# A list scheduler's rule for the port that VectorE and GpSimd share, and a new recorded order of the attention's blocks

## The chip, the core and the metric

One core of a Trainium2 chip runs one launch of the program. The metric is the device time of that launch in microseconds. Engines are named as in the profile: PE is TensorE's matmul, PEld its weight load, DVE is VectorE, ACT is ScalarE, POOL is GpSimd, SP is SyncE, which issues most of the DMAs.

## What is computed

The reference is one inference step of a two-layer decoder trunk with model width 1024, on 512 prompt positions and 8 sequences of 8 sample positions, all in float32. Cut to what matters:

```python
for l in range(DEPTH):                                   # 2 layers
    sh1, sc1, g1, sh2, sc2, g2 = ada_mod(c, ada_w[l], ada_b[l], 6)
    h = modulate(rms_norm(x, norm_g[l, 0]), sh1, sc1)
    if l < N_A_LAYERS:
        out, nbuf, h_last = recurrent_block(h, ...)      # conv, gates, linear recurrence
    else:
        q = apply_partial_rope((h @ attn_w_q[j]).reshape(B, T, N_HEADS, HEAD_DIM), pos)
        out = sliding_sink_attention(q, k_all, v_all, attn_sinks[j], p0) @ attn_w_o[j]
    x = x + g1[:, None, :] * out
    h = modulate(rms_norm(x, norm_g[l, 1]), sh2, sc2)
    x = x + g2[:, None, :] * swiglu(h, ffn_w_in[l], ffn_w_out[l])
    if l == N_A_LAYERS - 1:
        kv = (modulate(rms_norm(x, kv_norm_g), kv_shift, kv_scale) @ w_kv)   # keys, values
y = rms_norm(x, final_g)
```

## The kernel before

**Tiling.** The stream x is kept transposed in SBUF in two halves, A (h = 0) and B (h = 1); each half has 256 prompt columns and 32 sample columns, 288 in all, in 8 chunks of 128 rows. Float32 accuracy is made from three products in float32r: a value is split into hi (a rounding cast on ACT) and lo (value minus hi, a subtraction on DVE, now and then on POOL). So every weight block of 128 columns is loaded into a `raw` tile, cast by ACT into a `wh` tile and subtracted by DVE into another (`convert`, `operand`); a product of 8 row blocks is 24 matmuls of 128x288. Four `raw` tiles and ten `wh` tiles exist.

**Stages.** Recurrent block of layer 0 (about 30 to 250 us of the span), feed-forward of layer 0 (to about 640), shared keys and values (to about 690), attention with the q projection and the beginning of the output projection (about 690 to 820), rest of the output projection (to about 870), feed-forward of layer 1 and final norm (to the end). Beside these, matmuls for the conditioning vectors run in groups of 16 (tile `ada`) until about 608 us. Each feed-forward takes its first three column blocks plainly; the other 19 are done in pairs of halves with seven products where a plain product needs eight (`ffn` from line 1177, with `steps` at 1219 and `seven` at 1289). For these, POOL computes sums of weight quarters in place in `raw`: in one step S1 needs one sum, S2 two and S4 one (`operand`, which then casts on ACT and subtracts on DVE). With 19 steps in two layers these are 152 sums of 128x512 on POOL. S4 also has one product of 128x288 on POOL.

**Order of the work.** Nothing is issued while the program text runs. Each operation is recorded (`Engine.record`, lines 388 to 447; all instructions therefore stand at line 447 in the profile) with its engine, an estimated cost in ns, its operands and a `port` class. `Recorder.schedule` (from line 213) then simulates the five engines once and writes out one fixed order for each engine, which the chip follows: an engine's instructions run in that order, and each waits for its operands by semaphores. In each round the simulation takes, for every engine, the available operation with the smallest `s + 0.75 * prio`, where `s` is its simulated earliest start and `prio` its place in the recorded order, looking at up to 24 operations; of the engines' picks the one that starts first is placed. Tiles from rings (`raw`, `wh`, `sl`, `ta`, `tb`, `td`, the PSUM banks `mm` and `ada`) are given out in the same pass.

**The port.** Line 404 marks an operation that, in the model, uses a port which DVE and GpSimd share: a POOL operation that reads a wide SBUF operand, and a DVE operation that reads no PSUM and has two wide SBUF inputs or is a `tensor_scalar`. Class 1 is the usual case; class 2 (line 405) is a POOL operation of at most 40 elements. `port` holds the simulated end of the last class 1 operation (line 333). A class 1 operation on DVE may start 130 ns before that end; one on POOL starts 20 ns after it (line 302), whichever engine held the port before. So when both engines have a class 1 operation waiting behind a DVE operation, DVE's next one starts first in the simulation, and POOL's is put off again until DVE has nothing for the port.

**The attention.** `ATT` (line 53) is a list of blocks which the attention stage records one after another: `q0A` is q projection unit 0 of half A (24 matmuls and the rotary step; unit weights are converted at first use and released when both halves are done), `a0A` one chunk of two heads (4 or 8 score matmuls, masks with maximum on DVE, exponentials on ACT, a normalisation on ACT, DVE and POOL; its second part, transposes, the product with the values and a split, is put off by `flush(1)` until the next `a` or `s` block), `s0A` one sample sequence (`attn_sample`, with two DMAs for its cached keys and values), `fA` the end of a half's attention (`attn_fin`: flush, `k_out` with its small output DMAs, and the split of the sample columns that every output projection unit of that half reads), `o0A` unit 0 of the output projection. After the list come the other output units.

Of the kernel before, what the change touches and what calls it, by code (L numbers as in the profile page):

```python
# [49 lines left out]
WIN = 600  # L50

RNN = "x0 x1 x2 g0 g1 x3 y0 y1 x4 g2 g3 x5 y2 x6 y3 g4 g5 x7 y4 y5 g6 g7 y7 y6"
ATT = ("q0A q2A a0A q1A q0B a2A a1A q1B q3A a0B q2B a1B q4A a3A a4A q3B a2B q5A q4B a3B q6A a5A q5B q7A a6A a4B s0A "
       "q6B a5B s1A s2A s3A q7B a7A s0B a6B fA s2B a7B s1B o0A s3B o1A fB o2A")
LOOK = {"PE": 24, "DVE": 24, "ACT": 24, "POOL": 24, "SP": 24}
NRAW = 4
NSL, NTA, NTB, NTD = 37, 7, 8, 4
# [71 lines left out]
class Recorder:  # L129
# [83 lines left out]
    def schedule(self):  # L213
        import bisect

        last = {}
        for op in self.ops:
            for n in op.tiles:
                if n in self.kind_of:
                    last[n] = last.get(n, 0) + 1  # L220
            op.npred = len(op.preds)
            op.ready = 0.0
            for q in op.preds:
                q.succ.append(op)
        rel_at = {n: 0.0 for n in last}
        engs = ("PE", "DVE", "ACT", "POOL", "SP")
        avail = {e: [] for e in engs}
        free = {e: 0.0 for e in engs}
        slots = {k: [0.0] * c for k, (c, _) in self.kinds.items()}
        nxt = {k: 0 for k in self.kinds}  # L230
        got = set()
        cold = 0.0


        port, mode = 0.0, 0
        pos = {n: j for k in self.order for j, n in enumerate(self.order[k])}
        used = {n for n in last}
        table = [next(j for j, (n, _) in enumerate(TABLES) if n == "silu")]
        dma_free = [0.0]
        out = []  # L240

        def push(op):
            bisect.insort(avail[op.eng], (op.prio, op.i, op))

        for op in self.ops:
            if op.npred == 0:
                push(op)

        def alloc_time(op, now):
            t = 0.0  # L250
            need = {}
            for n in op.allocs:
                if n in got:
                    continue
                k = self.kind_of[n]
                sl = slots[k]
                i = need.get(k, 0)
                need[k] = i + 1
                o = self.order[k]
                while nxt[k] < len(o) and (o[nxt[k]] in got or o[nxt[k]] not in used):  # L260
                    nxt[k] += 1

                j, at = nxt[k], i
                while at and j + 1 < len(o):
                    j += 1
                    at -= o[j] not in got and o[j] in used
                m = i + (o[j] != n) * self.kinds[k][1]
                if len(sl) <= m:
                    return None
                t = max(t, sorted(sl)[m])  # L270
            return t

        n_left = len(self.ops)
        sp = deque(o.i for o in self.ops if o.eng == "SP")
        rest = deque(sorted(self.ops, key=lambda o: o.prio))
        done = set()
        while n_left:
            best = None
            while sp and sp[0] in done:
                sp.popleft()  # L280
            sp_next = sp[0] if sp else 0
            while rest[0].i in done:
                rest.popleft()
            limit = rest[0].prio + WIN
            for e in engs:
                f = free[e]
                pick = None
                seen = 0
                for pr, i, op in avail[e]:
                    if e == "SP" and i > sp_next + SPW:  # L290
                        break
                    if pr > limit:
                        break
                    at = alloc_time(op, f) if op.allocs else 0.0
                    if at is None:
                        seen += 1
                        if seen > LOOK[e]:
                            break
                        continue
                    s = max(f, op.ready, at)  # L300
                    if op.port == 1:
                        s = max(s, port - 130 if e == "DVE" else port + 20)
                    if e == "PE" and op.mode != mode:
                        s = max(s, f + 100)
                    sw = e == "ACT" and op.func and op.func not in FREE_FUNCS and (table[0] is None or op.func not in TABLES[table[0]][1])
                    if sw:
                        s = max(s, f + 1283)
                    key = (s + (SWW if sw else 0) + BETA * pr, pr)
                    if pick is None or key < pick[0]:
                        pick = (key, s, op, sw)  # L310
                    seen += 1
                    if seen > LOOK[e]:
                        break
                if pick and (best is None or pick[1] < best[1]):
                    best = pick
            if best is None:
                raise RuntimeError("no instruction can go: " + str({e: [(o.i, o.allocs) for _, _, o in avail[e][:3]] for e in engs}) + str({k: len(v) for k, v in slots.items()}))
            _, s, op, sw = best
            e = op.eng
            avail[e].remove((op.prio, op.i, op))  # L320
            if sw:
                table[0] = next(j for j, (_, fs) in enumerate(TABLES) if op.func in fs)
            for n in op.allocs:
                if n in got:
                    continue
                k = self.kind_of[n]
                c = [u for u in slots[k] if u <= s] or slots[k]
                slots[k].remove(max(c) if c is not slots[k] else min(c))
                got.add(n)
            op.start = s  # L330
            cost = op.cost
            if op.port == 1:
                port = s + cost
            elif op.port == 2 and s + 60 < port:
                cost += port - s
            if e == "PE":
                mode = op.mode
            if e == "PE":
                if s - free[e] > 3400:
                    cold = s + 3400  # L340
                if s < cold:
                    cost *= 2
            if op.lat:

                free[e] = s + op.cost
                b = max(s + op.cost + 650, dma_free[0])
                dma_free[0] = b + op.lat
                op.end = b + op.lat + 1700
            else:
                op.end = free[e] = s + cost  # L350
            for n in op.tiles:
                if n in last:
                    last[n] -= 1
                    rel_at[n] = max(rel_at[n], op.end)
                    if last[n] == 0:
                        slots[self.kind_of[n]].append(rel_at[n] + (260 if self.kind_of[n] in ("mm", "ada") or e == "PE" else 150))
            for q in op.succ:
                q.npred -= 1
                q.ready = max(q.ready, op.end + DELAY[op.eng][q.eng])
                if q.npred == 0:  # L360
                    push(q)
            out.append(op)
            done.add(op.i)
            n_left -= 1
        out.sort(key=lambda o: (o.start, o.i))
        return out
# [107 lines left out]
def trunk_kernel(ctx, tc, a):  # L474
# [1292 lines left out]
    each = []  # L1767
    for w in ATT.split():
        h, n = "AB".index(w[-1]), int(w[1:-1] or 0)
# [227 lines left out]
```

## Time and profile before

| what | before |
|---|---|
| median of 3 runs | 1275.53 us (1274.91 to 1280.13) |
| the profiled execution's own time | 1275.33 us |
| its span, first to last instruction | 1273.5 us |
| granted TensorE clock, mean | 0.993 |
| PE busy | 1246.1 us (98%) |
| PEld busy | 1172.8 us (92%) |
| DVE busy | 905.7 us (71%) |
| ACT busy | 659.4 us (52%) |
| POOL busy | 488.2 us (38%) |

All engines run at once, so the shares don't add up to one. An operation that waits for the port shows in the profile as a longer operation, not as idle time before it; an operation that waits for a semaphore shows as idle time with the engine and tile that released it.

### The profile page before, as it was taken

How to read it: one execution, taken by the hardware profiler on the slowest of the kernel's cores; microseconds unless marked ns; L12 is line 12 of the kernel's file. 1: busy time of each engine (PE TensorE's matmuls, PEld its weight loads, DVE VectorE, ACT ScalarE, POOL GpSimd, SP SyncE). 2: the span in 40 equal slices, each digit the busy share in tenths (PEclk: the TensorE clock that was granted, in tenths of full speed). 3: DMA queues.
4: the chain of work that ended last, by engine and by line, in shares of the span. 5: the costliest groups of instructions: out<-in, count | busy, mean ns of one | idle time of the engine just before them, and what ended most of it. 6: DMA issues, size and time to landing. Idle time of an engine off the chain costs nothing.

```text
span 1273.5 us, 25461 instructions
## 1 busy us (share of the span) xinstructions
PE 1246.1 (98%) x9568; PEld 1172.8 (92%) x9568; DVE 905.7 (71%) x2156; ACT 659.4 (52%) x1469; POOL 488.2 (38%) x709
## 2 busy tenths in 40 slices
PE   7999999999999999999999999999999999999997
PEld 5798899899998998999999997999999999999997
DVE  6988885775584686467578878558857758757856
ACT  4788873762352354145357768538424425524522
POOL 3476640131551552345024436110435345335511
PEclk8999999999999999999999999999999999999999
DMA  9956554416646556444432321322333323323232
GB/s 306 315 174 199 182 166 149 157 52 211 187 141 178 180 160 199 155 150 136 125 83 56 69 76 38 111 84 96 90 94 83 100 84 96 96 78 97 71 96 75
DMA packets 223981, 165.40 MB, mean 130 GB/s; under 512 B 23757, under 2 KB 209065, under 8 KB 223826
## 3 DMA queue, kind: packets, MB, share of 16 engines
q1 hardware_dynamic: 223410, 163.45, 42.5%
q8 instruction: 75, 1.23, 0.4%
q14 instruction: 48, 0.39, 0.1%
q0 software_dynamic: 448, 0.32, 0.1%
HBM read 160.85 MB, written 4.87 MB: 130 GB/s over the span
## 4 chain that ended last, share of the span: by engine, by line
PE 73%; DVE 13%; ACT 6%; POOL 4%; issue 2%; DMA 1%; SPq 0%; ACTq 0%; POOLq 0%; DVEq 0%
PE mm L447 69%; PE ada L447 4%; DVE wh L447 4%; DVE sl L447 4%; POOL raw L447 3%; ACT wh L447 2%; DVE ta L447 1%; DMA reg<-in_x_prompt_dram 1%; DVE td L447 1%; ACT tb L447 1%; ACT h L447 1%; ACT sl L447 1%; ACT ta L447 1%; DVE tb L447 1%; DVE h L447 1%
## 5 line engine op out<-in xcount | busy, mean ns | idle before, releaser
L447 PE MATMUL mm<-h,wh 128*128 128x288 f32 x4128 | 596.8, 299 | 3.5 <-ACT h L447 2.1
L447 PEld LDWEIGHTS mm<-h,wh 128*128 128x128 f32 x4128 | 562.4, 189 | 21.7 <-issue 9.9
L447 PE MATMUL mm<-sl,wh 128*128 128x288 f32 x3218 | 462.4, 296 | 0.8 <-ACT ta L447 0.8
L447 PEld LDWEIGHTS mm<-sl,wh 128*128 128x128 f32 x3218 | 436.9, 188 | 9.4 <-issue 5.9
L447 ACT CAST wh<-raw 128x512 fp32r<-128x512 f32 (+3 forms) x388 | 266.4, 710 | 292.4 <-PE mm L447 208.4
L447 DVE TENSOR_TENSOR wh<-raw,wh 128x512 fp32r<-128x512 f32 (+3 forms) x388 | 344.9, 913 | 60.1 <-ACT wh L447 54.0
L447 POOL TENSOR_TENSOR raw<-raw 128x512 f32<-128x512 f32 x76 | 109.8, 1445 | 183.9 <-DVE wh L447 154.1
L447 POOL TENSOR_TENSOR x<-x,ta 128x32 f32<-128x32 f32 x152 | 58.7, 386 | 306.8 <-DVE ta L447 306.7
L447 DVE SCALAR_TENSOR_TENSOR x<-mm,mods,x 128x256 f32<-128x256 f32 x160 | 77.3, 483 | 133.2 <-PE mm L447 132.1
L447 POOL TENSOR_TENSOR raw<-raw,raw 128x512 f32<-128x512 f32 x76 | 111.8, 1471 | 3.7
L447 PE MATMUL mm<-tb,wh 128*128 128x288 f32 (+1 forms) x488 | 89.7, 299 | 4.5 <-POOL sl L447 1.6
L447 PEld LDWEIGHTS mm<-tb,wh 128*128 128x128 f32 x488 | 72.3, 188 | 9.4 <-DVE td L447 5.4
L447 POOL TENSOR_TENSOR td<-td,td 128x288 f32<-128x288 f32 x38 | 32.0, 843 | 111.9 <-ACT td L447 106.5
L447 ACT ACTIVATE ta<-x 128x288 f32<-128x288 f32 x56 | 24.3, 443 | 67.2 <-POOL x L447 62.1
L447 PE MATMUL mm<-ta,wh 128*128 128x288 f32 (+1 forms) x254 | 55.9, 298 | 0.0
L447 DVE TENSOR_TENSOR td<-mm,td 128x288 f32<-128x288 f32 x76 | 33.2, 452 | 27.9 <-PE mm L447 27.9
L447 PE MATMUL ada<-reg,cz 128*32 128x512 f32 (+1 forms) x448 | 49.5, 553 | 0.0
L447 DVE TENSOR_TENSOR sl<-ta,sl 128x288 fp32r<-128x288 f32 x54 | 44.9, 834 | 1.7 <-ACT sl L447 1.5
L447 ACT COPY td<-mm 128x256 f32<-128x256 f32 (+1 forms) x102 | 34.2, 353 | 20.4 <-PE mm L447 18.4
L447 DVE TENSOR_TENSOR sl<-td,sl 128x288 fp32r<-128x288 f32 x50 | 38.2, 764 | 8.1 <-ACT sl L447 8.1
L447 ACT ACTIVATE ta<-mm 128x288 f32<-128x288 f32 x54 | 21.4, 410 | 43.2 <-PE mm L447 41.8
L447 PEld LDWEIGHTS mm<-ta,wh 128*128 128x128 f32 x254 | 41.5, 188 | 1.8 <-ACT wh L447 0.8
(202 smaller groups left out, 1248.4 us busy)
## 6 DMA issues: line engine op xcount, KB each, us to landing
raw<-in_ffn_w_in_dram SPq DMA_DIRECT2D x88, 512.0 KB
reg<-in_ada_w_dram SPq DMA_DIRECT2D x80, 512.0 KB
raw<-in_ffn_w_out_dram SPq DMA_DIRECT2D x32, 384.0 KB
raw<-in_ffn_w_out_dram SPq DMA_DIRECT2D x32, 320.0 KB
raw<-in_rnn_w_in_dram SPq DMA_DIRECT2D x16, 512.0 KB
reg<-in_kv_ada_w_dram SPq DMA_DIRECT2D x16, 512.0 KB
wh<-in_ada_w_dram SPq DMA_DIRECT2D x24, 256.0 KB
raw<-in_rnn_w_out_dram SPq DMA_DIRECT2D x8, 512.0 KB
```

The source lines that it names most:

```text
L447: self.rec.add(eng, lambda: getattr(obj, name)(*map(real, args), **{k: real(v) for k, v in kw.items()}), cost, outs, ins, func, lat, port, ...
```

## The change

Two edits in the scheduler and one in the recorded order. The scheduler now remembers which engine held the port last; a class 1 operation may start 100 ns before the port's end if the other engine held it, and 40 ns before if its own engine did. The latter never decides, since an engine's own last operation ends no earlier than that. With both engines waiting behind a DVE operation, POOL's now starts first in the simulation, then DVE's: they take turns. In `ATT`, `a1A` and `a1B` move behind `q4A` (`a1A` stood before `q1B`, `a1B` before `q4A`), `a4A` goes before `a3A`, `fA` and `s2B` go before `a6B`, and `fB` goes behind `o2A` as the last block. No operation is added or removed; every engine's fixed order in the whole program may come out differently.

```diff
-ATT = ("q0A q2A a0A q1A q0B a2A a1A q1B q3A a0B q2B a1B q4A a3A a4A q3B a2B q5A q4B a3B q6A a5A q5B q7A a6A a4B s0A "
-       "q6B a5B s1A s2A s3A q7B a7A s0B a6B fA s2B a7B s1B o0A s3B o1A fB o2A")
+ATT = "q0A q2A a0A q1A q0B a2A q1B q3A a0B q2B q4A a1A a1B a4A a3A q3B a2B q5A q4B a3B q6A a5A q5B q7A a6A a4B s0A q6B a5B s1A s2A s3A q7B a7A s0B fA s2B a6B a7B s1B o0A s3B o1A o2A fB"
...
-        port, mode = 0.0, 0
+        port, holder, mode = 0.0, "", 0
...
                     if op.port == 1:
-                        s = max(s, port - 130 if e == "DVE" else port + 20)
+                        s = max(s, port - 100 + (60 if holder == e else 0))
...
             if op.port == 1:
-                port = s + cost
+                port, holder = s + cost, e
             elif op.port == 2 and s + 60 < port:
                 cost += port - s
```

## Rows read from the trace of the kernel before

**Rows 1.** Stages: us, busy us by engine (instructions), granted clock, DMA share, GB/s.

```profile
0.00:60.00 60.00, 49.90 (x465) 36.52 (x466) 46.48 (x194) 34.95 (x82) 20.76 (x50) 0.91 1.02 311
60.00:160.00 100.00, 97.91 (x732) 87.58 (x733) 83.38 (x159) 85.62 (x162) 67.50 (x145) 1.00 0.57 188
...
700.00:820.00 120.00, 119.20 (x1033) 106.02 (x1032) 95.09 (x410) 86.41 (x296) 50.22 (x112) 1.00 0.26 70
...
915.00:1273.50 358.50, 350.53 (x2636) 347.11 (x2634) 252.51 (x492) 143.89 (x281) 139.64 (x149) 0.99 0.31 90
```

**Rows 2.** Waits of PE's weight loads, 60 to 160 us: releaser, us, times, longest.

```profile
PEld mm L447 <- POOL sl L447: 1.9, 1, 1.9
PEld mm L447 <- POOL tb L447: 1.4, 1, 1.4
```

**Rows 3.** The same, 700 to 820 us.

```profile
PEld mm L447 <- ACT ta L447: 1.6, 5, 0.5
PEld mm L447 <- DVE stat L447: 1.4, 6, 0.3
PEld mm L447 <- ACT td L447: 0.9, 3, 0.4
PEld mm L447 <- POOL ta L447: 0.8, 2, 0.5
```

**Rows 4.** The same, 820 to 915 us.

```profile
PEld mm L447 <- DVE wh L447: 0.7, 1, 0.7
PEld mm L447 <- DVE td L447: 0.6, 1, 0.6
```

**Rows 5.** The same, 915 to 1274 us.

```profile
PEld mm L447 <- DVE td L447: 3.5, 11, 0.5
```

**Rows 6.** DVE and POOL, 982 to 998 us: start, duration, operation, [idle before].

```profile
982.21 3.28 POOL L447 TENSOR_TENSOR raw<-raw,raw 128x512 f32<-128x512 f32 x2
984.27 1.54 DVE L447 TENSOR_TENSOR sl<-td,sl 128x288 fp32r<-128x288 f32 x1
...
991.75 1.28 POOL L447 TENSOR_TENSOR raw<-raw 128x512 f32<-128x512 f32 x1 [2.66 <-DVE wh L447]
...
993.71 0.69 DVE L447 TENSOR_TENSOR wh<-raw,wh 128x512 fp32r<-128x512 f32 x1 [1.31 <-ACT wh L447]
...
997.27 0.45 DVE L447 TENSOR_TENSOR mm<-mm,ta 128x288 f32<-128x288 f32 x1
```

**Rows 7.** DVE and POOL, 902 to 913 us.

```profile
905.54 5.17 DVE L447 TENSOR_TENSOR wh<-raw,wh 128x512 fp32r<-128x512 f32 x3
...
906.84 3.32 POOL L447 TENSOR_TENSOR raw<-raw,raw 128x512 f32<-128x512 f32 x2
910.23 1.63 POOL L447 TENSOR_TENSOR raw<-raw 128x512 f32<-128x512 f32 x1
```

**Rows 8.** POOL and DVE, 152 to 155 us.

```profile
152.31 0.37 POOL L447 COPY ta<-shT 128x4 f32<-128x4 f32 x1 [1.99 <-DVE ta L447]
153.59 1.06 POOL L447 COPY ta<-shT 128x4 f32<-128x4 f32 x1 [0.91 <-DVE ta L447]
...
153.37 1.22 DVE L447 TENSOR_TENSOR wh<-raw,wh 128x1024 fp32r<-128x1024 f32 x1
```

**Rows 9.** DVE subtractions into wh of 128x512: count, busy us, mean ns.

```profile
L447 DVE TENSOR_TENSOR wh<-raw,wh 128x512 fp32r<-128x512 f32 x266 | 214.6, 838 | 47.5 <-ACT wh L447 44.3
```

**Rows 10.** One stretch of the second feed-forward, columns as in rows 1.

```profile
1160.00:1180.00 20.00, 20.00 (x152) 19.79 (x151) 17.11 (x24) 11.08 (x23) 12.11 (x10) 1.00 0.38 106
```

**Rows 11.** Chain of waits, second feed-forward, one place in two successive steps.

```profile
1166.08 2.58 DVE sl L447 x2
...
1177.57 2.93 DVE sl L447 x2
```

**Rows 12.** DVE, 816 to 819 us, fB's end.

```profile
816.11 0.28 DVE L447 COPY sl<-mm 64x128 f32<-64x128 f32 x1 [0.86 <-PE mm L447]
...
818.60 0.41 DVE L447 TENSOR_TENSOR h<-sl,h 128x256 fp32r<-128x256 f32 x1
```

## The prediction, made before the changed kernel ran

> **What bounds the kernel now.** I read the busy time by stage first. PE is busy for 97.9 of 100 us in the recurrent stage, 119.2 of 120 in the attention and 350.5 of the last 358.5, at full granted clock nearly throughout [rows 1]; only the first 60 us differ, where the DMA engines are the full ones (share 1.02) and PE has 49.9. So the bound is PE's own stream, and a new order can win only the moments at which PE stands still for another engine. The reader finds them in the list of waits, in the rows of PE's weight loads: behind POOL 3.3 us in the recurrent stage [rows 2], in the attention 4.7 us in four groups of short waits of 0.5 us at most [rows 3], at the start of the second feed-forward 1.3 us [rows 4], and in its regular part 3.5 us in 11 waits of about 0.32 us [rows 5]. Together 12.8 us, 1% of the span: that is the ceiling of what I cost below.
>
> Then I looked for the port in the order of time. A DVE subtraction of 128x288 takes 1.54 us while POOL's pair of sums runs until 985.49; an operation of that size takes 0.45 alone, so it really began at 985.36, 0.13 us before POOL's end [rows 6]. The other way round: a POOL sum of 1.63 us takes 1.28 alone [rows 6], so it began at 910.58, 0.13 us before the end (910.71) of the subtractions it waited for [rows 7]. And they alternate: three subtractions took 1.72 us each where one alone takes 0.69, beside POOL sums of 1.66 [rows 6, 7]. One sum, one subtraction and two handovers give 1.28 + 0.69 - 0.26 = 1.71, so each subtraction waited for one whole sum. **The old model has one direction right** (DVE 130 ns before POOL's end) **and the other wrong**: it starts POOL 20 ns after DVE's end, 150 late, and therefore lets DVE go first again and again where the chip alternates. The new one is 30 ns off in both directions and alternates. It will plan DVE's operations in such a burst at the time they take.
>
> The Trainium skill, page "SBUF — State Buffer", section "A bandwidth-pool intuition that's wrong (but worth ruling out)", speaks against the new figure: it gives a GpSimd operation locked out by VectorE as blocked until VectorE's end plus about 115 ns. By it the old "20 after" would be nearer than the new "100 before", and this sum's gains would fall away. The two rows disagree with that for computing operations; the section measured descriptor writing.
>
> **The change part by part.** No instruction, DMA or operand changes, so the sum of work stays; what is moved is each engine's order. Sum against the profiled execution's 1275.33 us (span 1273.5 plus 1.8 around it), which lies 0.2 under the median of 1275.53.
>
> *Recurrent stage.* A tiny POOL copy of 0.37 us took 1.06, since a DVE subtraction of 128x1024 held the port from 153.37 to 154.59 [rows 8]; what it feeds leads to PE's two waits on POOL [rows 2]. With turns in the model such a subtraction is seen to delay POOL's chain, and the planner has reason to set it elsewhere. I take the 0.69 us at both waits: -1.4. Bounds: -3.3 (both waits gone) to +1.4 (two such copies blocked in addition).
>
> *Start of the second feed-forward.* Five or so sums run one after another against the subtractions, and PE waits 0.7 us for one of them and 0.6 for a copy behind [rows 4, 7]. The sums are needed too, so half of it: -0.7. Bounds: -1.3 to +1.0 (one more subtraction at 1.72 instead of 0.69).
>
> *Regular steps of the feed-forwards.* 11 waits for `td`, the PSUM additions that stand in DVE's queue behind port operations [rows 5]. DVE operations that need no port are now preferred while POOL holds it, because their simulated start is earlier. Four of the 11 waits: -1.3. Bounds: -3.5 to +3.5 (as many again). The first feed-forward has the same steps with `ada` groups between; none of its waits stands among the rows above, and I take nothing there.
>
> *Attention order.* `a1A` and `a1B` go behind `q4A`: four blocks later for `a1A`, so a pending second part of `a2A` is flushed by `a0B` instead, and the q units in between are converted and loaded earlier (two DMAs each on SP's queue, which has room at a DMA share of 0.26 [rows 1]). `s2B` before `a6B` issues its two cache loads earlier, also on SP. `fB` last puts its small output DMAs, and the split, behind `o2A`, and `o2A`'s 24 matmuls run under `s3B`'s chain. PE's waits there are short and many, on ACT and DVE, which are busy for 86 and 95 of 120 us [rows 1, 3]. A third of 4.7 us: -1.5. Bounds: -4.7, and +2.9, which is `fB`'s chain from 816.11 to 819.01 [rows 12] laid bare. `a4A` before `a3A` and `fA` before `a6B` swap neighbours under the same cover: nothing, hidden by q matmuls; if they aren't ready, one wait of at most 0.5 [rows 3].
>
> Sum: -1.4 - 0.7 - 1.3 - 1.5 = -4.9, so 1275.33 - 4.9 = **1270.4 us**. The ends add up to -12.8 and +8.8, or 1262.5 and 1284.1. About 0.5% (6.4 us) is what a measurement of this kernel can tell from no change, so the likeliest outcome lies within it.
>
> **The rivals.**
>
> *A: nothing to see.* The queues are fixed but PE's stream is so dense that shifts of 100 ns disappear in waits that exist anyway. For it: 119.2 of 120 us busy [rows 1]. Against it: alternation moves DVE's plan by 1 us an operation, not 100 ns. Also in this case, with a chance of 0.04 as the two rows stand against it: POOL really takes the port only after DVE's end, the plan gets worse by as much as I have it better, and the first three terms fall away: 1275.3 - 1.5 = 1273.8. The section of the Trainium skill above would have it so. Together 1274 to 1278, chance 0.22.
>
> *B: more than forecast.* All four groups of waits go, and some of the startup's 10 us of missing PE time [rows 1] with them: 1275.3 - 12.8 = 1262.5, or lower. For it: the attention's blocks may have been recorded in an order that suits only a wrong port. Against it: in the attention half of the waited time names ACT, which has no part in the port [rows 3]. Chance 0.13.
>
> *C: slower, DVE becomes the bound in the feed-forward's steps.* A step lasts 11.49 us [rows 11], and DVE is idle for 2.89 of 20 us there [rows 10], 1.66 per step. A contended subtraction costs 1.03 more than a free one; the mean of 266 is 0.838, so at present one in seven pays it [rows 6, 7, 9]. If the new order lines up two more with POOL's sums in a step, that is 2.06, over the room by 0.4 us, and PE waits for it in each of 38 steps: 15 us, 1290. In the 19 steps of the second feed-forward alone: 1283. It decides at 1.6 more per step. For it: the new model starts POOL's sums earlier and packs DVE's subtractions against them. Against it: on the chip both engines already start as soon as their semaphores allow, so the number of meetings need not grow. Chance 0.12.
>
> *D: slower, `fB`'s cover is gone.* `o0B` needs `fB`'s split and is recorded right behind it; with `o2A` in front, PE has only the next half A unit to put between. If it can't, the 2.9 us [rows 12] and the wait for `s3B` before it, as long again, are bare: +2 to +6 with the other terms won or not, 1275 to 1281. Chance 0.06.
>
> **How the numbers follow.** Forecast 0.47 (own range 1266 to 1274), A 0.22, B 0.13, C 0.12, D 0.06. Faster by over 0.5% means under 1269.1: B whole, and four tenths of the forecast (0.20): 0.33. Slower by over 0.5% means over 1281.9: C nearly whole, 0.12, and a little of D: 0.13. Within: 0.54. The range takes in the upper half of B and the lower end of C: 1261 to 1283; what is left out is some 0.04 below and 0.12 above.
>
> **What would show it.** Right: PE's waits on POOL in the recurrent stage shrink; the second feed-forward's waits for `td` fall below 3.5 us; subtractions of 128x512 average under 838 ns or stay, with DVE's PSUM additions earlier in each burst. In bursts the 1.7 us alternation stays, since the chip has it already. `fB`'s last split comes after `o2A`'s matmuls and PE shows no gap there. Wrong: the recurrent stage and the feed-forwards take the same time in the profile, and all the difference lies between 690 and 820 us; or the feed-forward's step grows beyond 11.49 us (C); or a new PE wait of some us on `h` before the first output unit of half B (D); or the clock is granted at half for a stretch where it was full.

## The result, and the profile after

The changed kernel takes 1264.49 us in the median of 4 runs (1262.62 to 1265.84), the kernel before 1276.53 in its 4 (1274.91 to 1280.13). The ratio is 0.9909, with a 95% interval of 0.9886 to 0.9933: 11.6 us faster, between 8.6 and 14.6. The profiled execution after took 1263.19 us (span 1261.4), the one before 1275.33 (span 1273.5), so the two traces differ by 12.1.

The ratios further down are each taken against runs of the kernel before from the same session, whose medians were 1275.88, 1275.85 and 1274.94 us.

The busy times, from the page of the changed kernel:

```profile
PE 1240.1 (98%) x9568; PEld 1170.2 (93%) x9568; DVE 889.4 (71%) x2156; ACT 649.2 (51%) x1463; POOL 494.7 (39%) x709
```

The work is the same (9568 matmuls, 2156 DVE and 709 POOL instructions), but DVE is busy for 16.3 us less than before (889.4 against 905.7). ACT has six instructions less, six loads of activation tables. The groups of instructions, before and after:

```profile
L447 ACT ACT_TABLE_LOAD x24 | 30.8, 1283 | 3.4 <-DMA raw<-in_c_sample_dram 3.0
```

```profile
L446 ACT ACT_TABLE_LOAD x18 | 23.1, 1283 | 7.2 <-DVE stat L446 3.9 <-DMA raw<-in_c_sample_dram 3.1
```

The new `ATT` is not needed for this: the rule alone (e1) also has 18 loads. Nor is it the turn as such, since e4 with turns has 24, and e3 and e10 without turns have 20 and 21.

The stages, in the view that answers to [rows 1]:

```profile
0.00:60.00 60.00, 51.06 (x482) 37.90 (x483) 47.60 (x195) 36.48 (x84) 23.57 (x52) 0.97 1.03 313
60.00:160.00 100.00, 99.35 (x742) 90.59 (x742) 84.76 (x156) 80.51 (x158) 65.56 (x135) 1.00 0.58 187
...
700.00:820.00 120.00, 119.04 (x1034) 105.98 (x1033) 92.19 (x403) 85.16 (x296) 47.86 (x106) 1.00 0.25 69
...
915.00:1261.40 346.40, 339.42 (x2570) 338.47 (x2568) 233.75 (x480) 140.79 (x274) 137.52 (x148) 0.99 0.31 89
```

PE stands still for 0.7 us in the recurrent stage's 100 (2.1 before), and hardly differently in the attention's 120. The last row is 12 us shorter, since all that was won before it moves its beginning.

And PE's waits from the recurrent stage, then those from 880 us to 1262 us, which answer to [rows 2, 4, 5]:

```profile
PEld mm L446 <- ACT ta L446: 1.4, 1, 1.4
...
PEld mm L446 <- DVE sl L446: 0.8, 1, 0.8
```

```profile
PEld mm L446 <- DVE td L446: 0.9, 1, 0.9
...
PEld mm L446 <- ACT td L446: 0.6, 1, 0.6
```

The waits on POOL in the recurrent stage are gone, and so are the 11 waits for `td` in the feed-forward's regular steps. What is left is at the entry of that stage: 0.9 for DVE's `td` and 0.6 for ACT's, about as much as the 1.3 of [rows 4].

Stages shift against each other, so a table says it better: the time between two marks in the trace, against the same marks in the trace before. A mark is the start of PE's n-th matmul of one kind: the 160th, 640th, 2000th and 2800th of `mm<-h,wh` (65, 150, 671 and 841 us), the 1600th, 1920th and 3200th of `mm<-sl,wh` (633, 936 and 1262 us), and a matmul of `ada<-td,sl` in the attention (744 us). The column heads are where the marks lie in the kernel before. All kernels of the study stand in it; those in the first group have turns in their rule for the whole program.

| kernel, us against before | to 65 | 65-150 recurrent | 150-633 | 633-671 keys | 671-744 attention | 744-841 attention, output | 841-936 | 936-1262 steps |
|---|---|---|---|---|---|---|---|---|
| changed kernel | -1.9 | -2.5 | +0.1 | -2.4 | -2.1 | -0.3 | +0.3 | **-3.4** |
| e1 rule only | +0.2 | -1.9 | -0.2 | -2.4 | -1.7 | +3.6 | -0.3 | **-3.8** |
| e4 POOL's side only | +1.3 | -0.2 | -1.0 | -3.5 | +0.2 | +12.6 | +0.7 | **-3.5** |
| e5 late turns | +3.9 | -2.3 | -2.6 | -1.5 | -1.6 | +3.3 | -2.6 | **-3.7** |
| e8 first half of order | -2.1 | -1.9 | -0.2 | -1.9 | -1.0 | +0.4 | -0.3 | **-3.3** |
| e9 second half of order | -1.5 | -1.9 | +0.1 | -2.4 | -1.7 | +4.0 | -0.3 | **-3.6** |
| e11 late turns, new order | +2.7 | -2.3 | -2.5 | -1.5 | 0.0 | +4.0 | -2.5 | **-4.1** |
| e7 135 ns, new order | +0.9 | +3.3 | +1.9 | -3.4 | -0.3 | +8.4 | -1.2 | **-3.4** |
| e13 late turns at the end | -1.6 | -1.9 | -0.3 | -2.4 | -2.1 | -0.3 | -1.1 | **-3.4** |
| e6 turns in 2nd feed-forward | -1.2 | 0.0 | +0.1 | -0.8 | 0.0 | 0.0 | -0.3 | **-3.9** |
| e12 by hand, old rule | -1.7 | -0.1 | +0.4 | 0.0 | 0.0 | 0.0 | -1.0 | **-2.6** |
| e3 control | -0.6 | -3.1 | +6.4 | +0.5 | -0.7 | +2.3 | 0.0 | **+0.5** |
| e10 control | -1.1 | +0.8 | -3.9 | +1.9 | +1.5 | +0.8 | +0.1 | **+0.1** |

The first row adds up to the 12.1 us; behind 1262 us only e13 differs from the kernel before (+0.7). The mark at 744 stands among blocks whose order differs between kernels. With a `mm<-h,wh` a microsecond earlier as the mark, e5 has +3.3 and -1.4 in the two columns of the attention in place of -1.6 and +3.3. Their sum is firm.

Two cells of the first row need care. The kernels e6 and e12 have the order of the kernel before up to the second feed-forward on every engine, and their rows show how far one execution differs from another of the same order: at most 0.4 us per stage from 65 to 841 us, but 0.8 in the keys' stage, and 1.2 and 1.7 us in the start. In the recurrent stage it can be 0.6: e1, e8, e9 and e13 have the changed kernel's order there and gain 1.9 where it gains 2.5. So the changed kernel's -1.9 in the start is hardly more than that, and up to 0.8 of its -2.4 in the keys' stage. What goes with the differences in the start and in the keys' stage is the granted clock; before, then e12, then e6, in stretches of 5 us:

```profile
20.00:25.00 5.00, 4.74 (x19) 3.45 (x19) 4.53 (x13) 3.42 (x7) 1.32 (x2) 0.50 1.11 341
25.00:30.00 5.00, 5.00 (x43) 3.25 (x41) 3.97 (x20) 2.35 (x6) 1.13 (x4) 0.50 1.10 349
660.00:665.00 5.00, 3.43 (x24) 2.96 (x22) 5.00 (x16) 5.00 (x14) 1.38 (x3) 0.99 0.00 0
665.00:670.00 5.00, 5.00 (x28) 4.65 (x28) 4.24 (x6) 5.00 (x11) 2.37 (x3) 0.67 0.53 113
```

```profile
20.00:25.00 5.00, 4.50 (x24) 3.02 (x23) 5.00 (x13) 3.44 (x7) 1.31 (x2) 0.82 1.11 341
25.00:30.00 5.00, 4.93 (x79) 3.17 (x82) 4.49 (x28) 2.62 (x7) 0.68 (x5) 1.00 1.10 348
660.00:665.00 5.00, 3.43 (x17) 2.75 (x17) 4.88 (x14) 5.00 (x13) 2.73 (x4) 0.85 0.00 1
665.00:670.00 5.00, 5.00 (x34) 4.88 (x34) 3.55 (x8) 4.03 (x7) 1.87 (x3) 0.81 0.88 190
```

```profile
20.00:25.00 5.00, 5.00 (x23) 3.84 (x22) 4.71 (x13) 3.51 (x7) 1.23 (x2) 0.54 1.12 339
25.00:30.00 5.00, 4.79 (x77) 3.21 (x77) 4.55 (x25) 2.61 (x7) 1.05 (x4) 1.00 1.10 349
660.00:665.00 5.00, 3.37 (x21) 2.57 (x19) 4.88 (x15) 5.00 (x13) 2.42 (x4) 1.00 0.00 0
665.00:670.00 5.00, 4.65 (x37) 4.48 (x36) 4.23 (x9) 4.35 (x7) 2.19 (x3) 1.00 0.80 170
```

The column behind the five engines is the clock. In the start PE ran at the lower of its two levels (0.50, 1.2 GHz) for all of the 10 us before, and for less in the two others. At 665 us, after a stretch in which PE had been busy for 3.4 of 5 us in all three, the clock fell in two and stayed at 1.00 in the third. A profile of this kernel is therefore worth some 2 us of luck, and the medians stand beside it below.

Other rows of the table hold such stretches too. The two longest, in e10 and in e7 (the kernel before has a mean clock of 0.89 from 660 to 675 us):

```profile
660.00:675.00 15.00, 13.91 (x68) 13.00 (x69) 9.89 (x22) 8.00 (x17) 6.61 (x7) 0.66 0.33 72
```

```profile
92.00:99.00 7.00, 5.67 (x23) 5.67 (x24) 3.84 (x12) 6.82 (x16) 0.45 (x1) 0.53 0.62 207
```

Shorter ones, at 0.66 for 5 us, lie in e5 (from 62 us), in e3 (from 173 and from 668), in e8 (from 663), in e7 (from 785) and in e4 (from 804), and in e9 one at 0.72 from 788 to 794. At 0.66 for 5 us, PE did the work of 3.3 us at most, so each of these can hold some 1.7 us of its cell; by the same estimate the one of e7 can hold all of its +3.3 in the recurrent stage. The stretch from 936 to 1262 us has none: the differences in its column are not the clock's.

### The profile page after: what moved, and what is told of

The parts are those of the page before. It is cut to its first block, busy times and chain, and to the rows that moved or that the text cites. A ratio compares the mean times of both kernels' runs of the same rounds, so it can differ in the third digit from the quotient of the medians.

```text
span 1261.4 us, 25458 instructions
## 1 busy us (share of the span) xinstructions
PE 1240.1 (98%) x9568; PEld 1170.2 (93%) x9568; DVE 889.4 (71%) x2156; ACT 649.2 (51%) x1463; POOL 494.7 (39%) x709
## 4 chain that ended last, share of the span: by engine, by line
PE 86%; DVE 5%; ACT 5%; DMA 2%; issue 1%; POOL 1%; SPq 0%; ACTq 0%; DVEq 0%
PE mm L446 82%; PE ada L446 4%; DVE sl L446 2%; DVE ta L446 1%; ACT sl L446 1%; ACT ta L446 1%; DVE wh L446 1%; DMA raw<-in_ffn_w_in_dram 1%; ACT h L446 1%; ACT tb L446 1%; DMA raw<-in_rnn_w_in_dram 1%; ACT wh L446 1%; DMA reg<-in_x_prompt_dram 0%; ACT L446 0%; DVE tb L446 0%
## 5 line engine op out<-in xcount | busy, mean ns | idle before, releaser
L446 ACT CAST sl<-ta 128x288 fp32r<-128x288 f32 x54 | 23.2, 433 | 28.4 <-DVE ta L446 28.3
L446 ACT ACTIVATE ta<-ta,stat 128x256 f32<-128x256 f32 (+2 forms) x72 | 32.5, 474 | 9.1 <-DVE stat L446 8.8
```

Of the source, the lines that this page charges most:

```text
L446: self.rec.add(eng, lambda: getattr(obj, name)(*map(real, args), **{k: real(v) for k, v in kw.items()}), cost, outs, ins, func, lat, port, ...
```

## The experiments

### The rule alone, a control, and the rule's two halves

e1 is the changed kernel with the old `ATT`. e3, e4 and e5 have the old `ATT` and another line in place of the rule:

```diff
-s = max(s, port - 130 if e == "DVE" else port + 20)
# e3
+s = max(s, port - 150 if e == "DVE" else port + 40)
# e4
+s = max(s, port - 130 if e == "DVE" else port - 100)
# e5, with holder recorded as in the change
+s = max(s, port + 20 if e == "POOL" else port - 130 if holder == "POOL" else port + 40)
```

Rule alone, expected:

> The new port rule with the attention's old order of blocks. Theory R (the rule brings the gain: DVE's operations are planned at the time they take, all over the program): PE is earlier by about 4 us at the end of the recurrent stage and gains about 3 us more in the second feed-forward, as in the changed kernel, and part of the 4.7 us between 608 and 830 us: 1264 to 1269 us. Theory O (the order of the attention brings the part between 608 and 830 us): 4 + 3 us gained and none there: about 1269 us, with the half-clock stretch near 665 us and PE's idle time at 690 to 700 us as before. Theory L (any new draw of the order moves the time by some us either way): no stage has to gain; 1264 to 1286 us.

Measured: 1268.11 us, ratio 0.9942 (0.9924 to 0.9959). The steps of the second feed-forward gain 3.8 us and the keys' stage 2.4, as in the changed kernel; between 744 and 841 us it loses 3.6. Theory R holds for the first two, theory O for the last. The 4 us that both expected by the end of the recurrent stage did not come (1.7 in the trace), nor did the half-clock stretch near 665 us that theory O expected. So the rule brings 7.4 us and the order of the blocks some 4 more.

Control, expected:

> A control: the old kind of rule with other wrong numbers (DVE 150 ns before the port's end, POOL 40 ns after it, DVE still first whenever both wait behind DVE), old order of blocks. Theory R: no better than before, 1274 to 1282 us, with PE's waits for td in the second feed-forward as before (3.5 us). Theory L: a new draw like any other, it may lie as low as 1264 us.

Measured: 1283.49 us, ratio 1.0055 (1.0035 to 1.0076), slower than theory R's range. The steps are 0.5 us longer and keep their waits, which R asked for; but 6.4 us are lost between 150 and 633 us, a stretch in which the rule alone moves next to nothing. Any edit to the rule has the planner draw another order for the whole program, and such a draw costs or wins several us by itself (up to 1.7 of these 6.4 can be the clock).

POOL's side alone, expected:

> Only POOL's half of the rule: POOL may start 100 ns before the port's end, DVE 130 ns before it as in the kernel before; old order of blocks. Both take turns by it. Theory R: the turn is what counts and not 30 ns on DVE's side, so it is as the rule alone within 0.3%, with the second feed-forward's waits for td gone. Theory L: a third draw, it need not agree with the rule alone in any stage.

Measured: 1279.76 us, ratio 1.0031 (1.0017 to 1.0044). The steps gain 3.5 us, as R says of turns. In total the expectation is missed widely: 30 ns in DVE's number part this kernel from e1, and of the 11.7 us between their medians (1268.11 against 1279.76) the traces put 9 in the stretch from 744 to 841 us. PE's waits there, in e4:

```profile
PEld mm L447 <- ACT ta L447: 3.1, 7, 0.8
...
PEld mm L447 <- POOL ta L447: 2.2, 1, 2.2
```

The attention's short operations arrive late for PE here and there: seven from ACT by 0.8 us at most, one from POOL by 2.2 us. In all, PE's weight loads wait there for 13.7 us for other engines (741 to 850 us), where in the same stretch of the kernel before they wait for 5.9: 7.8 of the 12.6 us. Up to 1.7 can be the clock; the rest stays open.

Late turns, expected:

> Turns with the old wrong number: POOL starts 20 ns after the port's end as before, but DVE's next operation of class 1 behind one of its own may start only 40 ns after that end, so POOL's goes first when both wait; old order of blocks. It parts the two things that the change does. If the turn is what counts: the second feed-forward gains its 3 us, total 1266 to 1271 us. If the 120 ns at POOL's start are what counts: as before, 1274 to 1279 us, with waits for td.

Measured: 1268.51 us, ratio 0.9949 (0.9931 to 0.9967). With POOL's start as late as in the old model, but POOL first when both wait, the steps gain 3.7 us and the stretch before them 2.6. So the turn counts there and the 120 ns do not.

### The second feed-forward by itself

e6 uses the new rule only for operations recorded from the second feed-forward on (`op.i >= marks[1]`, a mark set where that stage begins), with the old rule and old order before:

```diff
+new = op.i >= self.marks[1]
-s = max(s, port - 130 if e == "DVE" else port + 20)
+s = max(s, port - 100 + (60 if holder == e else 0) if new else port - 130 if e == "DVE" else port + 20)
```

> The new rule for operations recorded from the second feed-forward on, the old rule and the old order of blocks before it. Theory R (the turn mends DVE's queue in the feed-forward's steps): PE's waits for td there are gone and the stage from about 870 us to the end is 3 to 6 us shorter, everything before it as in the kernel before: 1270 to 1273 us. Theory L (luck of the draw): that stage as before, 1274 to 1278 us.

Measured: 1274.24 us, ratio 0.9978 (0.9964 to 0.9992), with the profile of 1269.32 at the low end of its runs. The steps gain 3.9 us and all stages between 65 and 841 us are as before but for the clock: theory R, though the median lies a little over its range. The interval, 1 to 4.6 us, holds the 3.9 of the trace.

The second control:

```diff
-s = max(s, port - 130 if e == "DVE" else port + 20)
+s = max(s, port - 110 if e == "DVE" else port)
```

> A second control: DVE may start 110 ns before the port's end and POOL at that end, so DVE still goes first when both wait behind DVE, though POOL's number is 20 ns better; old order of blocks. Theory R: the second feed-forward as before, with some 3 to 5 us of waits for td; the attention free to fall either way: 1270 to 1284 us. Theory L: the second feed-forward as likely 3 us shorter as not.

Measured: 1274.02 us, ratio 0.9985 (0.9971 to 0.9998). The steps are as before (+0.1) and keep their waits, so with both controls against ten kernels with turns in this stage (-3.3 to -4.1) the draw is out there: **the turn shortens the steps, in whatever form it is planned**. PE's longest waits for another engine from 880 us on, in e3, e10 and e5:

```profile
PEld mm L447 <- DVE td L447: 4.6, 12, 0.6
```

```profile
PEld mm L447 <- DVE td L447: 3.3, 9, 0.6
```

```profile
PEld mm L447 <- ACT ta L447: 0.4, 1, 0.4
```

What the turn did in a step is seen in DVE's timeline. Before, from the end of one step, DVE and then POOL:

```profile
1166.00 1.19 DVE L447 TENSOR_TENSOR sl<-td,sl 128x288 fp32r<-128x288 f32 x1
1167.11 1.55 DVE L447 TENSOR_TENSOR sl<-ta,sl 128x288 fp32r<-128x288 f32 x1
1168.58 0.45 DVE L447 TENSOR_TENSOR mm<-mm,ta 128x288 f32<-128x288 f32 x1
1169.07 0.46 DVE L447 COPY td<-mm 128x288 f32<-128x288 f32 x1
1169.44 4.42 DVE L447 TENSOR_TENSOR wh<-raw,wh 128x512 fp32r<-128x512 f32 x5
1173.78 0.45 DVE L447 TENSOR_TENSOR td<-mm,td 128x288 f32<-128x288 f32 x1
```

```profile
1165.06 3.28 POOL L447 TENSOR_TENSOR raw<-raw,raw 128x512 f32<-128x512 f32 x2
```

After, the same place, DVE and then POOL:

```profile
1155.24 1.19 DVE L446 TENSOR_TENSOR sl<-td,sl 128x288 fp32r<-128x288 f32 x1
1157.22 0.47 DVE L446 TENSOR_TENSOR mm<-mm,ta 128x288 f32<-128x288 f32 x1 [0.79 <-PE mm L446]
1157.60 0.45 DVE L446 TENSOR_TENSOR sl<-ta,sl 128x288 fp32r<-128x288 f32 x1
1157.96 1.29 DVE L446 TENSOR_TENSOR wh<-raw,wh 128x512 fp32r<-128x512 f32 x2
1159.17 0.45 DVE L446 COPY td<-mm 128x288 f32<-128x288 f32 x1
1159.54 1.41 DVE L446 TENSOR_TENSOR wh<-raw,wh 128x512 fp32r<-128x512 f32 x1
1161.37 1.29 DVE L446 TENSOR_TENSOR wh<-raw,wh 128x512 fp32r<-128x512 f32 x2 [0.42 <-ACT wh L446]
1162.58 0.45 DVE L446 TENSOR_TENSOR td<-mm,td 128x288 f32<-128x288 f32 x1
```

```profile
1154.29 3.31 POOL L446 TENSOR_TENSOR raw<-raw,raw 128x512 f32<-128x512 f32 x2
1158.80 1.61 POOL L446 TENSOR_TENSOR raw<-raw 128x512 f32<-128x512 f32 x1 [1.20 <-DVE wh L446]
```

The same operations stand in another order. Before, `sl<-td,sl` and `sl<-ta,sl` followed each other, and each waited for one of POOL's two sums, which ended at 1168.34 (1.19 and 1.55 us for an operation of 0.45). After, the sum in PSUM (`mm<-mm,ta`, which needs no port) stands between them, POOL's second sum ends at 1157.60, and `sl<-ta,sl` takes 0.45. And the sum in PSUM starts as soon as PE has written its operand: DVE had been idle for 0.79 us, waiting for PE, where before it came to that sum without a pause from the two splits, late. The addition for which PE waited (`td<-mm,td` at 1173.78, behind five conversions of 4.42 us) inherited that lateness; after, there is room of 0.42 us in the conversions ahead of it.

The steps in which this happens are the steps with the waits. From 936 to 1262 us, `sl<-ta,sl` runs 17 times. In the kernel before it takes 1.54 or 1.55 us in 11 of them, and it is behind these 11 that PE waits for `td`, each time 7 to 9 us later; in the other six it takes 0.45 and PE does not wait. In the changed kernel it takes 0.45 in all 17, and in each of the two controls it is long in 11 again. The mean of `sl<-ta,sl` over the program, before, after and in the second control:

```profile
L447 DVE TENSOR_TENSOR sl<-ta,sl 128x288 fp32r<-128x288 f32 x54 | 44.9, 834 | 1.7 <-ACT sl L447 1.5
```

```profile
L446 DVE TENSOR_TENSOR sl<-ta,sl 128x288 fp32r<-128x288 f32 x54 | 26.3, 490 | 0.7 <-ACT sl L446 0.6
```

```profile
L447 DVE TENSOR_TENSOR sl<-ta,sl 128x288 fp32r<-128x288 f32 x54 | 45.3, 843 | 0.9 <-ACT sl L447 0.7
```

Is this one exchange the cause? e12 makes it by hand, under the old rule: in the second feed-forward, the lo subtraction of half A is recorded behind the next step's PSUM sum (`put_off` is true for it alone; `rest()` issues it, and `rec.hold` makes it wait for the sum).

```diff
 def whole(h, f, t, put_off=False):
     m = mid[h][f] = (sl(F32R), sl(F32R))
+    if put_off:
+        S.copy(m[0].r[:, 0:HC], t.f[:, 0:HC])
+        later.append((m, t))
+        return
...
 V.tensor_tensor(o, o, b["p1"].f[:, 0:HC], ALU.add)
+rec.hold = [o]
+rest()
+rec.hold = []
```

> Old rule, old order of blocks, no change before the second feed-forward. There one operation per step is recorded later by hand: the lo subtraction of half A's product (sl<-ta,sl) goes behind the next step's PSUM sum (mm<-mm,ta), so that DVE does the operation that needs no port while POOL holds it. Theory R in its narrow form (this one exchange in DVE's queue is what the turn brought there): PE's waits for td fall from 3.5 us to under 1 and the stage is 3 to 4 us shorter: 1271 to 1273 us. If the exchange is beside the point and the place of the conversions (wh<-raw,wh) matters: as before, 1274 to 1278 us, with the waits.

Measured: 1272.85 us, ratio 0.9988 (0.9974 to 1.0002): by time alone unclear. By the trace, the steps gain 2.6 us, and the waits for `td` from 880 us on fall to 1.8 us from the 4.1 of [rows 4, 5]:

```profile
PEld mm L447 <- DVE td L447: 1.8, 4, 0.6
```

The median lies in the range that was expected of this one exchange (1271 to 1273 us), the waits stay over the 1 us. So the exchange brings 2.6 us where the turn brings 3.4 to 3.9 in the same stretch, two thirds or more. The rest is in DVE's other operations: `sl<-ta,sl` is short in all 17 steps of e12 too, but its conversions (`wh<-raw,wh` of 128x512) take 858 ns in the mean against 838 before and 828 in the changed kernel, so part of the waiting at the port went over to them. Whether that is all of the rest was not tried.

### The order of the attention's blocks

e8 has the new rule and the first half of the new order (`a1A a1B` behind `q4A`, `a4A` before `a3A`); e9 the second half (`fA s2B` before `a6B`, `fB` last):

```diff
# e8
-a2A a1A q1B q3A a0B q2B a1B q4A a3A a4A q3B
+a2A q1B q3A a0B q2B q4A a1A a1B a4A a3A q3B
# e9
-s0B a6B fA s2B a7B s1B o0A s3B o1A fB o2A
+s0B fA s2B a6B a7B s1B o0A s3B o1A o2A fB
```

> The new rule with the first half of the new order of blocks (a1A and a1B behind q4A, a4A before a3A) and the old second half. If the first half brings the 4 us that the changed kernel has over the rule alone: 1264 us. If the second half (fA and s2B before a6B, fB last) does: 1268 us as the rule alone. If the two depend on each other and each is one more draw of the attention: anything from 1262 to 1280.

> The new rule with the second half of the new order of blocks and the old first half. If the second half brings the 4 us: 1264 us. If the first half does: 1268 us, as the rule alone. If fB's chain lies bare behind o2A: a PE wait of 2 to 3 us on h before the first output unit of half B, 1270 us or more.

Measured: e8 1265.37 us, ratio 0.9917 (0.9900 to 0.9934), e9 1269.93, ratio 0.9953 (0.9935 to 0.9971). From 744 to 841 us e8 stands at +0.4 as the changed kernel (-0.3), e9 at +4.0 as the rule alone (+3.6). **The first half brings the order's share, and the second half nothing that these traces can tell**: in e9 up to 1.7 us of the +4.0 can be the clock, and e8 and the changed kernel lie 0.7 apart. PE's wait on `h` before half B's first output unit is 0.3 us in e9, as in the kernel before; `fB`'s chain has cover behind `o2A`. The first 97 us of the stretch, in the rule alone and in the changed kernel:

```profile
738.00:835.00 97.00, 94.61 (x804) 83.46 (x804) 68.47 (x287) 63.69 (x216) 31.23 (x75) 1.00 0.25 72
```

```profile
735.00:832.00 97.00, 96.04 (x825) 86.54 (x824) 68.23 (x277) 62.25 (x209) 33.93 (x78) 1.00 0.26 74
```

From about the same mark on, PE does 21 matmuls more in 97 us (825 against 804).

Is the new order good in itself? With the old rule it has no plan at all: the simulation comes to a point where the PSUM banks `mm` and the `wh` and `td` tiles are all given out and no operation can go on. So there is no run of this pairing. e11 joins it to the late turns, e7 to turns of 135 ns, and e13 keeps the change and uses late turns from the second feed-forward on:

```diff
# e11
-s = max(s, port - 100 + (60 if holder == e else 0))
+s = max(s, port + 20 if e == "POOL" else port - 130 if holder == "POOL" else port + 40)
# e7
+s = max(s, port - 135 + (60 if holder == e else 0))
# e13: e11's line if op.i >= self.marks[1], else the change's
```

> Turns with POOL's old late start (20 ns after the port's end, DVE behind its own operation 40 ns after it) and the new order of blocks. If the new order of the attention is good in itself: it adds its 3 to 4 us to the late turns' 1268.5, 1264 to 1266 us. If it fits the new rule's plan alone: 1267 us or more.

Measured: 1271.50 us, ratio 0.9968 (0.9954 to 0.9982). Over the whole attention the trace stands at +4.0 us where late turns with the old order (e5) stand at +1.7. So of the two rules that ran with both orders, the new order helps the change's and not the other.

> The changed kernel with 135 ns in place of 100, the overlap that the trace shows in both directions. If a truer number plans better: 1262 to 1264 us. If the turn alone counts and the rest is the draw of the attention: the second feed-forward 3 to 4 us under the kernel before as in all kernels with turns, the attention anything; 1262 to 1276 us.

Measured: 1279.29 us, ratio 1.0034 (1.0023 to 1.0045), 3 us over the widest of what was expected. The steps gain 3.4, the attention's second part loses 8.4. The number nearer to the chip's handover makes the slowest kernel with turns but e4.

> The changed kernel with the late turns from the second feed-forward on, where they gained most in its steps and entry (5.1 us against 3.1 to 4.2): up to 1.5 us under the changed kernel, 1262 to 1264 us. If the gain at the stage's entry came from the state that the attention left, and not from the rule: as the changed kernel, 1264 to 1265 us.

Measured: 1263.71 us, ratio 0.9916 (0.9898 to 0.9935). The trace shows 1.4 us at the stage's entry (841 to 936: -1.1 against +0.3), of which 0.7 is lost again behind 1262 us; the times don't part it from the changed kernel (0.9909, 0.9886 to 0.9933). So no version was found that is surely faster than the change.

## Why the prediction was right and where it was not

The range (1261 to 1283) held the time, and faster was the right side. The forecast of 1270.4 was too slow by 6 us: it took 4.9 us off, the runs show 11.6. Its own range (1266 to 1274) missed; rival B had named 1262.5, but by other means. Most of the chance (0.54) lay on a difference too small to tell, and it came out as nearly twice that bound. That the range held owes something to luck: of the 12.1 us between the two traces, 1.9 lie in the start and 2.4 in the keys' stage, for which nothing was forecast.

**The reading of the port** stands: overlap in both directions, alternation, DVE's operations planned too short. But it weighed number and turn alike. In the steps the turn did it: e5 has it with the old number and gains as much there, e7 has a truer number, gains no more there and is slower than before as a whole. The page of the Trainium skill that I set against the change, "SBUF — State Buffer" (section "A bandwidth-pool intuition that's wrong (but worth ruling out)"), gives about 115 ns after VectorE's end, measured for descriptor writing. For these operations the trace has 0.13 us before that end [rows 6, 7]. In the steps the sign did not decide: a planned start 20 ns after the end (e5) shortens them too.

**The steps** were the term that was mis-sized: "Four of the 11 waits: -1.3". All 11 went, 3.4 us. The mechanism was the one named (operations that need no port go first while POOL holds it), but I costed it per wait and took a third without a reason, when a row gave the size: an operation that no longer pays 1.1 us at the port (1.54 against 0.45 in [rows 6]), against room of 0.3 us that PE lacked per wait. DVE's mean for `sl<-ta,sl` fell from 834 to 490 ns. Rival C, which feared DVE as the bound in these steps, had the right engine and the wrong sign: from 936 to 1262 us DVE was busy for 233.0 of 326 us, and in the same stretch of the changed kernel for 221.1 of 323:

```profile
936.00:1262.00 326.00, 324.97 (x2444) 322.08 (x2443) 233.01 (x445) 134.53 (x263) 134.45 (x139) 1.00 0.30 87
```

```profile
927.00:1250.00 323.00, 323.00 (x2447) 322.64 (x2446) 221.07 (x446) 134.57 (x263) 133.79 (x139) 1.00 0.30 88
```

**The recurrent stage**: -1.4 forecast, -2.5 in the trace, -1.9 in e1, e8 and e9 with the same order there, and PE's waits on POOL did go. That is no proof of the cause I gave. A control without turns (e3) gains 3.1 in the same stage, and e4 with turns gains 0.2, so the gain there is more likely a draw of the order than the turn. (e7 loses 3.3, but that can be the clock.) Five of the six table loads that fell away lay in this stage. The prediction did not look at them, and they do not settle it: of 14 loads there before, 9 are left in the changed kernel, 11 in e3, which gains 3.1, and 12 in e10, which loses 0.8.

**The start of the second feed-forward**: -0.7 forecast, +0.3 measured (841 to 936). The waits changed their names, as PE's waits from 880 us on show, and kept their length. Late turns do win 1.1 to 2.6 us there, and the exchange by hand (e12) 1.0; the change's rule does not.

**The attention**: -1.5 forecast for the new order, with no price for either half by itself (`a1A` passes five blocks, not four). In the trace the whole attention gains 2.4 us, but this is a sum of two things of which I saw neither: the rule loses 3.6 us from 744 to 841 with the old order (1.9 over the whole attention), and the first half of the order wins that back (e8 stands at -0.6 over the whole attention). I had taken waits that exist as the ceiling and not asked what a new rule does to an attention ordered for the old one. Rival D did not come: `fB` last costs nothing.

**Without a term**: 633 to 671 us, the keys' stage, gains 2.4, of which up to 0.8 is the clock. All nine kernels with turns in that stage gain there (1.5 to 3.5) and the two controls do not (+0.5, and +1.9 of which most can be e10's lower clock), so the turn is the likely cause; which operation it is was not tried. The first feed-forward was put at nothing and came out so (150 to 633: +0.1).

## What to carry to other kernels

When a planner's model of a shared resource is mended, look in the trace for who goes first when both wait, before the exact nanoseconds: here the turn is worth 3 to 4 us in one stage in every form, and the number nothing there. Such an edit also draws a new order everywhere else, and stages without a regular pattern moved by -4 to +9 us for 20 to 35 ns in the rule, the clock's share included; so compare stage by stage, run a control with other wrong numbers, and expect to fit the hand-made orders to the new plan again. A sum over PE's existing waits says what a better order can win; it does not say what is lost where the blocks had been ordered for the old plan (here 3.6 us from 744 to 841).

## What was not expected of the hardware

The stretch at the lower clock in the start varies from run to run of the same order (10 us at 0.50 before, 0.54 and then 1.00 in e6, 0.82 and then 1.00 in e12), and at 665 us the same idle share of PE was followed by a fall of the clock in two executions and by none in a third. Together that went with differences of 1.7 and 2.0 us between executions of the same order, more than each term that the prediction summed.
